# A seven-product scheme for the wide layers, with two of its weight sums made by accumulating DMAs

## The chip, the cores and the metric

One NeuronCore of a Trainium2 chip runs the program. The metric is the device time of one execution in microseconds, the median of several runs; a profile of one further execution gives the trace. TensorE is called PE, VectorE DVE, ScalarE ACT, GpSimd POOL and SyncE SP.

## The reference, cut to what matters

512 tokens of 1024 features go through two layers of a first block (projection, attention over selected keys, short convolution, gates, and an MLP) and then through a second block (projection, dilated attention, mLSTM, and a gated feed-forward network, here FFN). All is float32. The change touches the products of the MLP and of the FFN:

```python
for l in range(2):                                   # first block
    ...
    u = rmsnorm(x, norm_mlp[l])
    x = x + jnp.square(jax.nn.relu(u @ w_mlp_up[l])) @ w_mlp_down[l]   # 1024 -> 4096 -> 1024
...
h = modulate(rms_norm(x, g_ffn), sh_f, sc_f)          # second block
x = x + gt_f * ((jax.nn.silu(h @ w_gate) * (h @ w_up)) @ w_down)       # 1024 -> 2816 -> 1024
```

The vector by which the second block is modulated, `silu(c) @ w_ada + b_ada` with `w_ada` of 1024 x 6144, depends on none of this; the kernel computes it in pieces (`ada`) on DVE beside an MLP.

## The kernel before, in words

Activations are kept transposed: a tile has 128 features on the partitions and 512 tokens along the row, and x is eight such tiles. A large product is made exact enough by splitting both sides into two float32r parts. For the weights, `split` copies a raw tile of 4 x 128 rows by 256 columns (1024 elements in each partition) to `wh` on ACT (L171), and DVE subtracts that from the raw tile to get `wl` (L172). For the activations, `hilo` does the same with `hi` (L285, ACT) and `lo` (L286, DVE). Each block of 128 x 128 weights then takes three matmuls into one PSUM bank: wh by hi (L230), wh by lo (L231), wl by hi (L232). In the FFN, `gateup` has its own three (L1315 to L1317).

`linear` cuts a product into units (one split weight tile) and pieces (the matmuls of 128 output columns over 4 k-tiles of 128 rows), and calls an evacuation when a bank is complete. All pieces go into one list. `Prog.run` walks it in order: at a unit it emits the weight splits up to two units ahead, and a share of the background work ("bg", at "rate" pieces per unit; "drain" empties the rest); at a "do" it emits the work itself. A scheduler then orders the instructions of each engine, and every engine runs its own queue strictly in that order. Weights arrive on SP's queue in tiles of 1 MB (`fetch`, L161, three buffers). "Rate 0.8" lets the 48 `ada` pieces run as background in the MLP of layer 1.

The MLP goes in four chunks of 1024 hidden columns, in the order up 0, up 1, down 0, up 2, down 1, up 3, down 2, down 3. `rstd` comes after the first two pieces of up 0: a product of the square sums with a matrix of ones (L313), a root on ACT, a reciprocal and its refinement on DVE (L316 to L325). `evup` scales and clips on DVE (L732), squares on ACT (L733) and splits by `hilo`; `evdn` adds to x (L740), and after the last chunk `nextprep` splits x for the next stage. The last 512 output columns of layer 1 are made in two halves of 256 tokens (`parts_=2`), so that the norm of block 2 (L829 to L863) can begin on the first half. The FFN goes through `gateup` in groups of 256 columns, the first one in two token halves, and `down` in three chunks.

## Time and profile before

| | |
|---|---|
| median of 3 runs | 2069.94 us (2069.59 to 2069.95) |
| profiled execution | 2069.96 us, span 2067.9 us from first to last instruction |
| granted TensorE clock | 1.000 |
| PE busy | 2057.1 us, 99% of the span |
| DVE busy | 1260.0 us, 61% |
| ACT busy | 845.6 us, 41% |
| POOL busy | 19.7 us, 1% |
| HBM read | 211.55 MB |

How to read it: busy time is the union of an engine's instructions; a matmul's own duration overlaps the next one's, so what a matmul costs is the distance between two starts. A row of a timeline has the start and the length in us, the engine, the line of the kernel, the operation, its tiles (out<-in), its shape, and in brackets the idle time before it with what ended it. A group's row has the count, the busy time, and the mean of one in ns.

### The profile page before, as it was taken

What the parts mean: (1) busy time and instruction counts of PE and PEld (TensorE: products, weight loads), DVE (VectorE), ACT (ScalarE), POOL (GpSimd) and SP (SyncE); (2) the same over time, 40 slices, a digit from 0 to 9 for tenths busy, and PEclk for the clock granted to TensorE, in tenths of its full rate; (3) what the DMA queues carried; (4) which work ended last, traced back from release to release, by engine and by line L of the source; (5) the groups of instructions that cost most, each with busy time, mean ns of one, the idle gap of its engine ahead of it and who ended that gap; (6) DMA issues with size and microseconds to landing.
All of it is one profiled execution on the core that took longest, in us unless ns stands there. A gap on an engine that the chain in (4) does not pass through costs nothing.

```text
span 2067.9 us, 25080 instructions
## 1 busy us (share of the span) xinstructions
PE 2057.1 (99%) x9944; PEld 1700.7 (82%) x9944; DVE 1260.0 (61%) x2245; ACT 845.6 (41%) x1359; POOL 19.7 (1%) x33
## 2 busy tenths in 40 slices
PE   9999999999999999999999999999999999999999
PEld 7888888888888878888888888889877798888887
DVE  6999666644444569977657746567777375333333
ACT  5324773432322332238644322425377744322221
POOL 0000000000000000000000000000010000000000
PEclk9999999999999999999999999999999999999999
DMA  5222213233323222331134545452221123233231
GB/s 204 102 94 93 79 62 102 82 102 102 96 88 102 87 94 90 102 102 62 62 123 169 209 141 194 145 195 98 82 82 62 42 81 103 81 103 101 83 111 51
DMA packets 122148, 215.25 MB, mean 104 GB/s; under 512 B 5808, under 2 KB 30640, under 8 KB 122032
## 3 DMA queue, kind: packets, MB, share of 16 engines
q1 hardware_dynamic: 122032, 213.67, 30.9%
q8 instruction: 78, 1.28, 0.2%
q14 instruction: 38, 0.31, 0.0%
HBM read 211.55 MB, written 2.10 MB: 103 GB/s over the span
## 4 chain that ended last, share of the span: by engine, by line
PE 97%; DVE 1%; ACT 1%; issue 0%; DMA 0%; POOL 0%; SPq 0%; POOLq 0%; DVEq 0%; ACTq 0%
PE mm L230 25%; PE mm L232 25%; PE mm L231 25%; PE mm L1315 4%; PE mm L1317 4%; PE mm L1316 4%; PE at L352 1%; PE mm L260 1%; PE mm L261 1%; PE mm L262 1%; PE ot L386 1%; PE at L371 1%; PE at L1188 0%; PE at L1196 0%; PE at L582 0%
## 5 line engine op out<-in xcount | busy, mean ns | idle before, releaser
L230 PE MATMUL mm<-g,wh 128*128 128x512 f32 (+1 forms) x2400 | 919.5, 384 | 1.0 <-ACT wh L171 0.8
L232 PE MATMUL mm<-g,wl 128*128 128x512 f32 (+1 forms) x2400 | 916.0, 382 | 0.0
L231 PE MATMUL mm<-g,wh 128*128 128x512 f32 (+1 forms) x2400 | 915.4, 382 | 0.0
L171 ACT CAST wh<-raw 128x1024 fp32r<-128x1024 f32 (+2 forms) x356 | 366.4, 1032 | 825.8 <-PE mm L231 648.6
L172 DVE TENSOR_TENSOR wl<-raw,wh 128x1024 fp32r<-128x1024 f32 (+2 forms) x356 | 424.9, 1195 | 448.1 <-ACT wh L171 445.8
L230 PEld LDWEIGHTS mm<-g,wh 128*128 128x128 f32 x2400 | 450.4, 188 | 90.5 <-issue 4.3
L231 PEld LDWEIGHTS mm<-g,wh 128*128 128x128 f32 x2400 | 450.6, 188 | 86.3 <-issue 1.2
L232 PEld LDWEIGHTS mm<-g,wl 128*128 128x128 f32 x2400 | 450.7, 188 | 86.1
L1317 PE MATMUL mm<-g,wl 128*128 128x512 f32 (+1 forms) x384 | 142.6, 372 | 0.0
L1316 PE MATMUL mm<-g,wh 128*128 128x512 f32 (+1 forms) x384 | 142.4, 372 | 0.0
L1315 PE MATMUL mm<-g,wh 128*128 128x512 f32 (+1 forms) x384 | 142.2, 372 | 0.0
L286 DVE TENSOR_TENSOR g<-g,g 128x512 fp32r<-128x512 f32 x96 | 66.4, 691 | 49.7 <-ACT g L285 49.2
L285 ACT CAST g<-g 128x512 fp32r<-128x512 f32 x96 | 59.6, 621 | 60.6 <-DVE g L707 26.6
L1317 PEld LDWEIGHTS mm<-g,wl 128*128 128x128 f32 x384 | 72.3, 188 | 12.6
L1316 PEld LDWEIGHTS mm<-g,wh 128*128 128x128 f32 x384 | 72.3, 188 | 12.5
L1315 PEld LDWEIGHTS mm<-g,wh 128*128 128x128 f32 x384 | 72.1, 188 | 12.4
L740 DVE TENSOR_TENSOR x<-mm,x 128x512 f32<-128x512 f32 (+1 forms) x68 | 44.8, 658 | 56.5 <-PE mm L232 56.5
L803 DVE SCALAR_TENSOR_TENSOR g<-g,g 128x512 f32<-128x512 f32 x96 | 63.8, 688 | 8.6 <-DMA g<-w_ada 8.5
L733 ACT ACTIVATE g<-g 128x512 f32<-128x512 f32 x64 | 40.3, 630 | 70.1 <-DVE g L732 70.1
L360 ACT ACTIVATE g<-g,nm 128x128 f32<-128x128 f32 (+3 forms) x96 | 53.2, 555 | 17.8 <-DVE nm L355 17.1
L601 DVE MAX8 m<-g 128x8 f32<-128x256 f32 (+2 forms) x96 | 53.3, 558 | 1.9
L602 DVE MATCH_REPLACE8 g<-m,g 128x256 f32<-128x256 f32 (+2 forms) x96 | 52.1, 543 | 0.0
(222 smaller groups left out, 1574.4 us busy)
## 6 DMA issues: line engine op xcount, KB each, us to landing
raw<-w_in SPq DMA_DIRECT2D x53, 1024.0 KB, 5.0
raw<-w_mlp_up SPq DMA_DIRECT2D x32, 1024.0 KB, 5.4
raw<-w_mlp_down SPq DMA_DIRECT2D x32, 1024.0 KB, 5.1
g<-w_ada SPq DMA_DIRECT2D x96, 256.0 KB, 5.6
raw<-w_gate SPq DMA_DIRECT2D x11, 1024.0 KB, 5.1
raw<-w_up SPq DMA_DIRECT2D x11, 1024.0 KB, 5.2
raw<-w_down SPq DMA_DIRECT2D x10, 1024.0 KB, 5.0
raw<-w_mix_out SPq DMA_DIRECT2D x8, 1024.0 KB, 5.1
```

What stands on the lines that cost most here:

```text
L171: act.copy(hi, raw)
L172: dve.tensor_sub(lo, raw, hi.bitcast(F32))
L230: pe.matmul(ps, wh, hi[:, cs], start=st, stop=False)
L231: pe.matmul(ps, wh, lo[:, cs], start=False, stop=False)
L232: S["pe"] = pe.matmul(ps, wl, hi[:, cs], start=False, stop=en)
L285: act.copy(hi, src)
L286: dve.tensor_sub(lo, src, hi.bitcast(F32))
L601: dve.max(m8, acc[i][:, :W_])
L803: dve.scalar_tensor_tensor(w, w, 1.0, S["cb", n2], op0=ALU.mult, op1=ALU.mult, accum_out=modp[:, n2, n : n + 1])
L1315: pe.matmul(ps, wh, hi[:, cs], start=s == 0 and k_ == 0, stop=False)
L1316: pe.matmul(ps, wh, lo[:, cs], start=False, stop=False)
L1317: pe.matmul(ps, wl, hi[:, cs], start=False, stop=s == 1 and k_ == 3)
```

## The change

`seven` computes a block of 1024 rows by 512 weight columns as seven half-sized products in place of eight (the Strassen-Winograd form). The 1024 rows are cut into two halves and the 512 columns into two: four quarters a, b, c, d of 512 x 256; the tokens are cut into two halves of 256. Each of the seven products multiplies one quarter, or one sum of quarters, by one half of the tokens, or a mixture of them: 4 k-tiles x 2 column tiles x 3 matmuls of 256 columns. `mix` makes the eight mixture tiles (`ta`, `tb`) once for each MLP and for the FFN, as background work on DVE. Four sums of weights are needed in each block: a plus c (`ac`) and c plus d (`cd`) arrive by loading one quarter on SP's queue and adding the other onto the same tile with a DMA on POOL's queue; then DVE adds a (`p5`) and b (`p2`) to `cd` in place. The results are combined while they are evacuated (`e6`, `e7`, `keep`).

The blocks are 1 to 7 of eight in the up-projection of each MLP, and 2 to 10 of eleven in the FFN, where gate and up columns take the places of the two column halves: 23 in all. Their pieces are meshed with those of `down`, which now takes 512 hidden rows at a time, with weight tiles of 128 columns (`narrow`). Loads are cut to 0.5 MB and requested five units ahead (eight buffers), the `ada` pieces are spread over both layers, 24 each, at rate 0.25, and the rope tables are loaded per layer.

```diff
-    prog = Prog(split, 2)
+    prog = Prog(fetch, split, 5, 2)
...
+    def seven(srcs, xs, ta, tb, evac):
...
+        def of(name):
+            W, c0 = srcs["cd".count(name)]
+            r0 = 512 * "bd".count(name)
+            return W[r0 : r0 + 512, c0 : c0 + 256].rearrange("(k p) c -> p k c", p=P)
+
+        def get(*names):
+
+            def f():
+                for name in names:
+                    raw[name] = (ssp if name == "cd" else rawp).tile([P, 4, 256], F32, tag="ws" if name == "cd" else "raw", name=nm("raw"))
+                    nc.sync.dma_start(raw[name], of(name[0]))
+                    for more in name[1:]:
+                        nc.gpsimd.dma_start(raw[name], of(more), accum_op=ALU.add)
+            return f
+
+        def p5():
+            dve.tensor_add(raw["cd"], raw["cd"], raw["a"])
+
+        def p2():
+            dve.tensor_add(raw["cd"], raw["cd"], raw["b"])
+
+        us = {
+            1: {"load": get("a", "cd"), "make": lambda: raw["a"]},
+            5: {"load": get("b"), "make": lambda: raw["cd"], "post": p5},
+            6: {"load": get("ac"), "make": lambda: raw["cd"]},
+            2: {"load": get("d"), "make": lambda: raw["b"], "post": p2},
+            7: {"make": lambda: raw["ac"]},
+            3: {"make": lambda: raw["cd"]},
+            4: {"make": lambda: raw["d"]},
+        }
...
+        def e6():
+            u = tmp.pop(1)
+            dve.tensor_sub(u, bank["Y"], u)
+            dve.tensor_sub(bank["Z"], bank["Z"], u)
+            act.copy(bank["Y"], u)
...
+        def e7():
+            r = tmp.pop(5)
+            dve.tensor_sub(r, bank["Y"], r)
+            evac(1, 1, r, True)
...
+        prods = [
+            (1, "X", half(xs, 0, 0), keep(1, "X")),
+            (5, "Z", half(ta, 0, 0), keep(5, "Z")),
+            (6, "Y", half(tb, 0, 0), e6),
+            (2, "X", half(xs, 4, 0), e2),
+            (7, "Y", half(ta, 0, 1), e7),
+            (3, "Z", half(xs, 4, 1), e3),
+            (4, "Y", half(tb, 0, 1), e4),
+        ]
...
+                    ps = bank[b][:, th(m)]
+                    for k in range(4):
+                        hi, lo = mv(k)
+                        wh = u["hi"][:, k, m * P : (m + 1) * P]
+                        wl = u["lo"][:, k, m * P : (m + 1) * P]
+                        pe.matmul(ps, wh, hi, start=first and m == 0 and k == 0, stop=False, skip_group_check=True)
+                        pe.matmul(ps, wh, lo, start=False, stop=False, skip_group_check=True)
+                        S["pe"] = pe.matmul(ps, wl, hi, start=False, stop=k == 3, skip_group_check=True)
...
+    def mix(key, k, y):
...
+        def first():
+            y0, y1 = y(k), y(k + 4)
+            a_, b_ = st["a"], st["b"] = slot(), slot()
+            dve.tensor_sub(a_[:, th(0)], y0[:, th(0)], y0[:, th(1)])
+            dve.tensor_add(b_[:, th(0)], y1[:, th(1)], a_[:, th(0)])
+            dve.tensor_sub(a_[:, th(1)], y0[:, th(1)], y1[:, th(1)])
+            dve.tensor_sub(b_[:, th(1)], y1[:, th(0)], b_[:, th(0)])
...
+        def evup(c):
+            def f(n, t, src, own):
+                r = src if own else slot()
+                dve.scalar_tensor_tensor(two(r), two(src), 0.0, both(S["n", "rs"][:, th(t)]), op0=ALU.max, op1=ALU.mult)
                 S["act"] = act.activation(r, r, AF.Square)
-                hid[c, 4 * g + j] = hilo(r)
+                for m in range(2):
+                    k_ = 4 * c + 2 * n + m
...
+                    act.copy(hi[:, th(t)], r[:, th(m)])
+                    dve.tensor_sub(lo[:, th(t)], r[:, th(m)], hi[:, th(t)].bitcast(F32))
...
-        u0 = up(0)
+        u0 = linear(W_up, 0, [4, 4], 0, [P] * 4, xs, ev0)
         add(u0[:2])
         do(lambda: rstd("n"))
-        if l == 1:
-            do(ada_start)
-            I.append(("rate", 0.8))
-            I.append(("bg", [ada(n) for n in range(48)] + [ada_end]))
+        I.append(("rate", 2.5))
+        I.append(("bg", [f for k in range(4) for f in mix("n", k, y)]))
         add(u0[2:])
-        add(up(1))
-        add(down(0))
...
+        I.append(("drain", None))
+        do(ada_start)
+        I.append(("rate", 0.25))
+        I.append(("bg", [ada(n) for n in range(24 * l, 24 * l + 24)] + ([ada_end] if l else [])))
+        for c in range(1, NU):
+            I.extend(mesh(up(c), down(c - 1)))
...
+        u0 = gateup(0, 2)
...
+        I.append(("rate", 2.0))
+        I.append(("bg", [f for k in range(4) for f in mix("h", k, y)]))
+        add(gateup(1, 1))
+        I.append(("drain", None))
+        for c in range(2, NG - 1, 2):
+            I.extend(mesh(unit(c) + unit(c + 1), down(c // 2 - 1)))
+        I.extend(mesh(unit(NG - 1), down(ND - 2)))
+        add(down(ND - 1))
```

In the changed file the split is at L218 (both halves of `linear`'s three matmuls at L279 to L281), `hilo`'s low half at L456, `mix` at L476 to L479, `ev0` at L928, the three matmuls of `seven` at L401 to L403, and the accumulating DMA at L329.

Before, PE's queue in the MLP of layer 0 holds plain products of 512 columns. These rows are the third 128 columns of the second half of up 0 (numbers are the program's tile numbers, `g` are activations in halves):

```order
L230 MATMUL mm_3466<-g_3050,wh_3388 128x512
L231 MATMUL mm_3466<-g_3051,wh_3388 128x512
L232 MATMUL mm_3466<-g_3050,wl_3389 128x512
L230 MATMUL mm_3466<-g_3068,wh_3388 128x512
L231 MATMUL mm_3466<-g_3069,wh_3388 128x512
L232 MATMUL mm_3466<-g_3068,wl_3389 128x512
```

Now PE's queue has this a little later in that MLP, in the first `seven`: `mm_3648` and `mm_3700` are its products 5 and 6, `g_3570` and `g_3574` the high halves of the last mixtures `ta` and `tb`, `at_3630` the first tile of `down`, `g_3547` and `g_3566` the last two hidden tiles of `ev0`.

```order
L401 MATMUL mm_3700<-g_3518,wh_3644 128x256
L402 MATMUL mm_3700<-g_3519,wh_3644 128x256
L403 MATMUL mm_3700<-g_3518,wl_3645 128x256
L279 MATMUL at_3630<-g_3547,g_3510 128x512
L280 MATMUL at_3630<-g_3548,g_3510 128x512
L281 MATMUL at_3630<-g_3547,g_3511 128x512
L279 MATMUL at_3630<-g_3566,g_3510 128x512
L401 MATMUL mm_3648<-g_3570,wh_3586 128x256
L280 MATMUL at_3630<-g_3567,g_3510 128x512
L281 MATMUL at_3630<-g_3566,g_3511 128x512
L401 MATMUL mm_3700<-g_3574,wh_3644 128x256
```

Products of the mixtures and of the first hidden tiles alternate there, each with operands that DVE has just made.

DVE's queue at that place before the change: the end of `rstd`, then evacuations (L732), low halves (L286) and weight splits (L172).

```order
L324 SCALAR_TENSOR_TENSOR g_3305<-g_3306,g_3305 128x512
L325 SCALAR_TENSOR_TENSOR g_3307<-g_3305,g_3307 128x512
L732 SCALAR_TENSOR_TENSOR g_3362<-mm_3277,g_3307 128x512
L286 TENSOR_TENSOR g_3366<-g_3362,g_3365 128x512
L732 SCALAR_TENSOR_TENSOR g_3381<-mm_3290,g_3307 128x512
L172 TENSOR_TENSOR wl_3433<-raw_3430,wh_3432 128x1024
```

And now, the end of that stretch of DVE's queue, ahead of the operands in PE's rows:

```order
L456 TENSOR_TENSOR g_3515<-g_3463,g_3514 128x512
L456 TENSOR_TENSOR g_3519<-g_3464,g_3518 128x512
L476 TENSOR_TENSOR g_3526<-g_3522 128x256
L477 TENSOR_TENSOR g_3527<-g_3524,g_3526 128x256
L478 TENSOR_TENSOR g_3526<-g_3522,g_3524 128x256
L479 TENSOR_TENSOR g_3527<-g_3524,g_3527 128x256
L928 SCALAR_TENSOR_TENSOR g_3544<-mm_3411,g_3380 128x512
L456 TENSOR_TENSOR g_3548<-g_3544,g_3547 128x512
L928 SCALAR_TENSOR_TENSOR g_3563<-mm_3424,g_3380 128x512
L456 TENSOR_TENSOR g_3567<-g_3563,g_3566 128x512
L456 TENSOR_TENSOR g_3571<-g_3526,g_3570 128x512
L456 TENSOR_TENSOR g_3575<-g_3527,g_3574 128x512
```

From the first of `rstd`'s DVE instructions to the last of these, `g_3575`, DVE's listing has 44 rows: 16 of `mix`, 12 low halves, 4 wide weight splits, 2 weight sums, a narrow split, 4 evacuations and 5 of `rstd`.

POOL's queue had casts of the attention (L412 then, L600 now) and some memsets; now the accumulating DMAs stand between. The rows are those from the end of layer 0's MLP to the attention of layer 1; `raw_9853` and `raw_10432` are the `cd` tiles of layer 1's first two blocks.

```order
L329 DMA raw_5717<-w_mlp_up 128x4x256
L329 DMA raw_6024<-w_mlp_up 128x4x256
L329 DMA raw_6143<-w_mlp_up 128x4x256
L329 DMA raw_9853<-w_mlp_up 128x4x256
L329 DMA raw_10432<-w_mlp_up 128x4x256
L600 COPY g_7054<-g_7054 64x512
```

So these two sums of layer 1 are issued before its attention, with an SP load ahead of each.

## Rows read from the trace of the kernel before

**Rows 1.** the page: span, busy time by engine; the chain by engine
```profile
span 2067.9 us, 25080 instructions
...
PE 2057.1 (99%) x9944; PEld 1700.7 (82%) x9944; DVE 1260.0 (61%) x2245; ACT 845.6 (41%) x1359; POOL 19.7 (1%) x33
...
PE 97%; DVE 1%; ACT 1%; issue 0%; DMA 0%; POOL 0%; SPq 0%; POOLq 0%; DVEq 0%; ACTq 0%
```

**Rows 2.** products by shape: xcount | busy us, mean ns | idle before
```profile
L230 PE MATMUL mm<-g,wh 128*128 128x512 f32 x2192 | 858.8, 392 | 0.8 <-ACT wh L171 0.8
...
L1315 PE MATMUL mm<-g,wh 128*128 128x512 f32 x320 | 124.5, 389 | 0.0
...
L230 PE MATMUL mm<-g,wh 128*128 128x256 f32 x192 | 54.4, 286 | 0.2 <-ACT g L860 0.2
...
L1315 PE MATMUL mm<-g,wh 128*128 128x256 f32 x64 | 17.7, 284 | 0.0
```

**Rows 3.** timeline of PE, 1100 us: start, length; ends of 24 steps
```profile
1100.22 0.39 PE L230 MATMUL mm<-g,wh 128*128 128x512 f32 x1
...
1105.66 0.39 PE L230 MATMUL mm<-g,wh 128*128 128x512 f32 x1
```

**Rows 4.** timeline of PE at 1439 us: first and last of 35 steps
```profile
1439.03 0.28 PE L232 MATMUL mm<-g,wl 128*128 128x256 f32 x1
...
1443.23 0.28 PE L232 MATMUL mm<-g,wl 128*128 128x256 f32 x1
```

**Rows 5.** timeline of DVE at 1100 us, layer 1: start, length, operation, [idle before]
```profile
1100.92 0.69 DVE L286 TENSOR_TENSOR g<-g,g 128x512 fp32r<-128x512 f32 x1
1101.53 0.69 DVE L732 SCALAR_TENSOR_TENSOR g<-mm,g 128x512 f32<-128x512 f32 x1
1103.57 0.69 DVE L286 TENSOR_TENSOR g<-g,g 128x512 fp32r<-128x512 f32 x1 [1.35 <-ACT g L285]
...
1132.22 1.22 DVE L172 TENSOR_TENSOR wl<-raw,wh 128x1024 fp32r<-128x1024 f32 x1
1133.36 0.68 DVE L803 SCALAR_TENSOR_TENSOR g<-g,g 128x512 f32<-128x512 f32 x1
```

**Rows 6.** timeline at 1412 us: 256-column work, then the border
```profile
1412.43 0.42 DVE L740 TENSOR_TENSOR x<-mm,x 128x256 f32<-128x256 f32 x1
...
1412.76 0.41 DVE L307 TENSOR_TENSOR g<-g,g 128x256 f32<-128x256 f32 x1
...
1415.54 0.58 PE L829 MATMUL at<-rdc,g 128*128 128x1 f32 x4
...
1421.50 0.48 DVE L863 SCALAR_TENSOR_TENSOR g<-g,modc,g 128x256 fp32r<-128x256 f32 x1
```

**Rows 7.** high half of a split on ACT: xcount, mean ns
```profile
L171 ACT CAST wh<-raw 128x1024 fp32r<-128x1024 f32 x342 | 359.6, 1053 | 802.8 <-PE mm L231 627.4 <-PE mm L1316 81.0 <-issue 71.4
```

**Rows 8.** stretches: length, then busy PE, PEld, DVE, ACT, POOL; clock, DMA, GB/s
```profile
65.00:235.00 170.00, 169.95 (x762) 140.74 (x760) 153.33 (x303) 61.84 (x89) 2.45 (x4) 1.00 0.30 99
415.00:700.00 285.00, 285.00 (x1259) 236.07 (x1258) 120.19 (x136) 89.78 (x109) 0.00 (x0) 1.00 0.30 98
1125.00:1415.00 290.00, 290.00 (x1332) 242.40 (x1331) 175.90 (x322) 93.00 (x118) 0.32 (x1) 1.00 0.50 174
```

**Rows 9.** timeline of DVE where the MLP of layer 0 begins
```profile
374.36 0.69 DVE L316 TENSOR_SCALAR g<-at 128x512 f32<-128x512 f32 x1 [0.77 <-ACT g L315]
...
381.61 0.69 DVE L732 SCALAR_TENSOR_TENSOR g<-mm,g 128x512 f32<-128x512 f32 x1
```

**Rows 10.** timeline of PE at the same place
```profile
371.27 1.02 PE L313 MATMUL at<-g,kon 128*128 128x512 f32 x2
```

**Rows 11.** busy time in slices where the FFN begins
```profile
1720.00:1730.00 10.00, 10.00 (x72) 9.39 (x71) 6.56 (x11) 4.64 (x8) 0.00 (x0) 1.00 0.29 93
1730.00:1740.00 10.00, 10.00 (x46) 8.28 (x45) 2.45 (x2) 2.11 (x2) 0.00 (x0) 1.00 0.37 119
```

**Rows 12.** DMA issues: xcount, KB each, median us from issue to landing
```profile
raw<-w_mlp_up SPq DMA_DIRECT2D x32, 1024.0 KB, 5.4
```

More of the change, by code (lines that the diff above doesn't have):

```diff
@@ L26 @@
 FF2 = 2816
+MLP_TILES = 32
+FF_TILES = FF2 // P
 C_NMIX, C_NMLP, C_NFIN, C_GMIX, C_GFFN = 0, 16, 32, 40, 48
@@ L48, with __init__ @@
 class Prog:
-    def __init__(self, split, ahead):
+    def __init__(self, fetch, split, early, ahead):
         self.items = []
+        self.fetch = fetch
         self.split = split
+        self.early = early
         self.ahead = ahead
@@ L64, in run @@
             if kind == "unit":
+                while got < len(units) and got <= cur + self.early:
+                    self.fetch(units[got])
+                    got += 1
                 while nxt < len(units) and nxt <= cur + self.ahead:
@@ L98, in interleave, with mesh @@
     return out
+def mesh(a, b):
+    n = len(a)
+    out = []
+    for i, x in enumerate(a):
+        out.extend(x)
+        for p in b[i * len(b) // n : (i + 1) * len(b) // n]:
+            out.extend(p)
+    return out
 @with_exitstack
@@ L162, in fetch, with granule @@
         return raw
-    def split(u):
-        chunk, k0, kn, cc0, ccn = u["src"]
-        if id(chunk) not in raws:
-            raws[id(chunk)] = fetch(chunk)
-        raw = raws[id(chunk)][:, k0 : k0 + kn, cc0 : cc0 + ccn]
-        hi = whp.tile([P, kn, ccn], F32R, tag="wh", name=nm("wh"))
-        lo = whp.tile([P, kn, ccn], F32R, tag="wl", name=nm("wl"))
+    def granule(u):
+        ch, k0, kn, cc0, ccn = u["src"]
+        W, r0, kt, c0, cw = ch
+        if kt * cw <= GRAN:
+            return (id(ch), 0, 0), (W, r0, kt, c0, cw)
+        gw = min(max(ccn, GRAN // kn), cw - cc0 // (GRAN // kn) * (GRAN // kn))
+        g0 = cc0 // (GRAN // kn) * (GRAN // kn)
+        return (id(ch), k0, g0), (W, r0 + k0 * P, kn, c0 + g0, gw)
+    def fetch(u):
+        if "load" in u:
+            u["load"]()
+        if "src" in u:
+            key, what = granule(u)
+            if key not in raws:
+                raws[key] = load(*what)
+    def split(u):
+        if "make" in u:
+            raw = u["make"]()
+            kn, ccn = raw.shape[1:]
+        else:
+            ch, k0, kn, cc0, ccn = u["src"]
+            key, what = granule(u)
+            k0, cc0 = (k0, cc0) if key[1:] == (0, 0) and what[2] * what[4] == ch[2] * ch[4] else (0, cc0 - key[2])
+            raw = raws[key][:, k0 : k0 + kn, cc0 : cc0 + ccn]
+        if u.get("narrow"):
+            hi, lo = (slot(F32R, kn * ccn).rearrange("p (k c) -> p k c", k=kn) for _ in range(2))
+        else:
+            hi = whp.tile([P, kn, ccn], F32R, tag="wh", name=nm("wh"))
+            lo = whp.tile([P, kn, ccn], F32R, tag="wl", name=nm("wl"))
         act.copy(hi, raw)
@@ L203, in linear @@
             ch = chunk(W, row0 + kbase * P, kt, c0, cw)
-            us = halves(ch)
+            us = halves(ch, narrow)
             steps.append((kbase, kt, us))
@@ L237, in linear, with th, two, both @@
                         first = False
+        return pieces
+    def th(t):
+        return slice(t * H, (t + 1) * H)
+    def two(ap):
+        return ap.rearrange("p (n c) -> p n c", n=2)
+    def both(ap):
+        return ap.unsqueeze(1).to_broadcast([P, 2, H])
+    def seven(srcs, xs, ta, tb, evac):
+        raw = {}
+        bank = {}
+        tmp = {}
+        def of(name):
[23 more added lines that the diff above has]
+        }
+        def half(d, k0, t):
+            return lambda k: [o[:, th(t)] for o in d(k0 + k)]
+        def keep(n, b):
+            def f():
+                tmp[n] = slot()
+                act.copy(tmp[n], bank[b])
+            return f
+        def e6():
[3 more added lines that the diff above has]
+            act.copy(bank["Y"], u)
+        def e2():
+            evac(0, 0, bank.pop("X"), False)
+        def e7():
+            r = tmp.pop(5)
+            dve.tensor_sub(r, bank["Y"], r)
+            evac(1, 1, r, True)
+        def e3():
+            evac(0, 1, bank.pop("Z"), False)
+        def e4():
+            evac(1, 0, bank.pop("Y"), False)
+        prods = [
[7 more added lines that the diff above has]
+        ]
+        pieces = []
+        for n, b, mv, after in prods:
+            first = n in (1, 5, 6)
+            u = us[n]
+            piece = [("unit", u)]
+            for m in range(2):
+                def emit(u=u, b=b, mv=mv, m=m, first=first):
+                    if first and m == 0:
+                        bank[b] = mmbank()
+                    ps = bank[b][:, th(m)]
[6 more added lines that the diff above has]
+                        S["pe"] = pe.matmul(ps, wl, hi, start=False, stop=k == 3, skip_group_check=True)
+                piece.append(("do", emit))
+            piece.append(("do", after))
+            pieces.append(piece)
@@ L1351, in down, with y @@
             p = []
[L1352 removed]
+            kt = min(4, FF_TILES - 4 * c)
+            last = c == ND - 1
             for g in range(2):
[L1354 removed]
+                p += linear(a["w_down_2"], 512 * c, [kt], 512 * g, [P] * 4, lambda k_: ff[4 * c + k_], evff(c, g),
+                            narrow=not last, newbank=mmbank if last else atbank)
             def free():
[L1357 to L1358 removed]
+                for k_ in range(kt):
+                    ff.pop(4 * c + k_)
             p.append([("do", free)])
             return p
[L1363 removed]
+        def y(j):
+            t = slot()
+            hi, lo = S["h", j]
+            dve.tensor_add(t, hi.bitcast(F32), lo.bitcast(F32))
+            return t
+        u0 = gateup(0, 2)
         add(u0[:8])
```

165 lines of the change are left out of this document (102 added, 63 removed).

## The prediction

> **What bounds the kernel now.** I read the page first: TensorE (PE) is busy for 2057.1 of the 2067.9 us of the span, and the chain that ended last is 97% PE [rows 1]. So only fewer or shorter products, or new waits of PE, can move the time. Second, the products by shape: most have 512 moving columns, the rest here 256 [rows 2]. Their means (392 and 286 ns) overlap in the pipeline, so the price is the distance between starts. At 1100 us, 24 steps take 5.44 us, 0.2267 us each [rows 3]. At 1439 us, 35 steps with 256 columns take 4.20 us, 0.120 us each [rows 4]. Two half products cost 0.240 us, 6% more than a whole one. Third, the stretches: in both MLPs PE never idles, while VectorE (DVE) is busy for 120 of 285 us and 176 of 290 us, ScalarE (ACT) for 90 and 93; the granted clock is 1.00 throughout [rows 8]. The new work must fit into that DVE and ACT room. That DVE can be full without hurting PE is seen in the attention stretch (153.3 of 170 us, PE 169.95) [rows 8], but that work was not all awaited by PE.
>
> **The products.** A block of 1024 rows by 512 columns takes 96 products of 512 columns now: 96 x 0.2267 = 21.76 us. `seven` takes 7 x 24 = 168 of 256 columns: 168 x 0.120 = 20.16 us. The gain is 1.60 us, not an eighth (2.72), since halves are dearer. There are 23 such blocks (7 in each layer, 9 in the FFN): 36.9 us. Around them 48 more whole products stay in 512 columns that ran as 96 halves, since fewer pieces are cut in two token halves (-0.6 us). In sum 2160 products of 512 and 96 of 256 columns go, 3864 of 256 come: -489.7 - 11.5 + 463.7 = **-37.5 us**.
>
> The rows give 226.7 and 120.0 ns [rows 3, 4]. The Trainium skill (TensorE: Matmul & The Clock Gate, Back-to-back issue gap) gives the isolated gap as N/2.4 + 2.5 ns, 215.8 and 109.2 ns; by it the sum would be about -54.7 us. The trace has 11 ns more on either shape, which weighs double on halves, so I keep the rows.
>
> **The steady iteration.** One `seven` meshed with one `down` piece of 512 hidden rows keeps PE for 20.16 + 21.76 = 41.9 us. DVE by distance between starts: 1.14 us for 1024 wide (1132.22 to 1133.36), 0.61 for 512 (1100.92 to 1101.53) [rows 5], 0.33 for 256 [rows 6], of which I take 0.36. Seven splits and two sums of weights 10.3; eight narrow splits 4.9; e6 and e7 1.8; `evup` 4 x 0.61 + 8 x 0.36 = 5.3; eight adds to x 4.9; 3.4 pieces of ada at two 0.61 each 4.2: 31.4 us of 41.9. ACT has seven casts of 1.05 [rows 7] and some 22 shorter operations, about 20 us. Both fit. But DVE waits in order: where a result makes the round trip DVE, ACT, DVE with nothing between, it idles 1.35 us [rows 5]. Following the order of one iteration, the narrow splits come just in time. I take 0.15 us per iteration, **+2 us** for 14 (bounds 0 and 7).
>
> **The start of each MLP** is the dearest new wait. Before, DVE needs only the four evacuations there. Now, between the reciprocal root and the first `seven`, the same queue carries `mix`, weight sums and `ev0`. In layer 0 DVE starts on it at 374.36; the root takes 7.25 us to 381.61, 1.14 of it a split [rows 9], so 6.1. Then come 16 operations of 256 columns (5.8), 12 low halves of 512 (7.3), 4 splits and 2 sums of 1024 (6.8), a narrow split (0.6), and 4 evacuations (2.4): with the root 29.0 us, to 403.4 without a gap. Four round trips, at up to 1.35 us [rows 5], add 5: 408.4. PE finishes the rstd products at 372.3 [rows 10], then has 72 products of 0.2267 (to 388.6), 58 of 0.120 and 12 of 0.2267 (to 398.3), where the listing has it wait for the last `ta` and `tb` from DVE. The wait is 5 us without gaps and 10 with them. Queued behind it on PE are the `down` products, which wait for `ev0` in the same DVE queue, so nothing can fill the hole. I take 10 for each layer, **+20 us** (bounds 10 and 24), since the evacuations there are the same round trips as that in [rows 5].
>
> **The borders.** Layer 1 to block 2: the second token half of the last `down` covers the norm of the first. Eight pieces of 12 x 0.120 are 11.5 us now; with four k instead of eight, 5.8. The first normalised tile takes from 1415.54 to 1421.98 [rows 6], 6.4 us, and seven more follow: about +2.5. Layer 0 to 1: in the last `down` a tile of x is finished every 2.72 us, in place of four close together, a pause, and four more; DVE needs some 2.4 us for each (add, low half, square sum, half a split), which leaves little to catch up with: +1.5. Together **+4 us** (0 to 9).
>
> **The start of the FFN.** `mix` takes 8 adds, 16 short operations and 8 low halves, 15.6 us, plus 4.6 for the first `seven`'s splits and sum; DVE idles 3.4 + 7.6 = 11 us in the 20 us concerned [rows 11]. The surplus of 9 is partly covered by the first product, which needs no mixture, and the `down` pieces between: **+3 us** (0 to 8).
>
> **Loads.** An iteration moves 5 x 0.5 MB by plain loads and 2 x 0.5 by accumulating ones, 2 MB for `down` and 1.7 for ada: 7.2 MB in 41.9 us, 172 GB/s, which layer 1 sustains now (174, PE full) [rows 8]. No accumulating transfer stands in the trace. The nearest row is a 1 MB load, 5.4 us to landing [rows 12]. `ac` is requested five units (of 2.8 us) ahead of product 6 and cast for product 7 some seven units later, 20 us; minus the load 15 are left for the sum. `cd` is requested far earlier, as POOL's listing shows. Even at twice a load both are hidden, so I take 0 (bounds 0, and what the second rival gives). POOL itself is 1% busy [rows 1].
>
> **Sum**: -37.5 + 2 + 20 + 4 + 3 = -8.5 us against the profiled execution's 2069.96 (span 2067.9 and 2.1 around it; the median of the runs is 2069.94, the same): **2061.5 us**. All lower bounds give -27.5 (2042.5), all upper ones +10.5 (2080.5).
>
> **Rivals.** *The full gain*: DVE gets to `mix` early enough, or the round trips fill each other, and the starts cost under 5 us each. For it: some low halves run without any gap, as the one at 1100.92 [rows 5], and the listing mixes the chains. Against: 29 us of work stand in a window of 24 (374.36 to 398.3). Time 2032 to 2042. *DVE becomes the bound of every iteration* (slower): four evacuations and eight late narrow splits, each followed by an idle of 0.8 to 1.35 us, add 10 to 12 us to the 31.4 and the iteration takes 43 to 44.5 instead of 41.9. It decides from 42.5 (8.5 us over 14); at 44.5 it costs 36 instead of 2: 2096. For it speaks the idle of 1.35 [rows 5]; against it that ada and splits stand between the steps of a round trip in the listing. *The accumulating sum is late*: every us beyond the 15 stops ACT's cast, the squares queued behind it, and so PE, 23 times. Landing at 16 us instead of 15 takes +23 (2084); the point is 15.4. Against: 5.4 us for a plain load of twice the size [rows 12].
>
> The Trainium skill (SBUF — State Buffer, SBUF: two separate sides) warns that a DMA issued from GpSimd starves while DVE runs a two-port operation. Its section Who interferes with whom says that tensor_tensor has no two-port mode, and by that rule the DVE work here would not delay the sums. No run here shows either yet.
>
> **Chances.** The forecast with its bounds (2042.5 to 2080.5) 68%: 54 faster, 9 within 0.2% (2065.8 to 2074.1, about what a measurement here can tell from no change), 5 slower. Full gain 12%, DVE the bound 13%, late sums 7%. So faster 0.66, same 0.09, slower 0.25. The range 2039 to 2084 leaves out half of the first rival and most of the other two, about 18%.
>
> **What would show it.** Right: 3864 products at L401 to L403, 0.120 us apart; a hole of about 10 us on PE, ahead of L401 and L279, waiting for L456, some 26 us after the rstd products of each MLP, and hardly any PE idle in the later iterations; accumulating transfers landing within 10 us; PE idle of 1 to 5 us at the two borders and the FFN's start. Wrong: no hole at the starts (then 2042 or less); PE idle repeated in every iteration with DVE named (then above 2080); PE waiting for casts that wait for a POOL transfer; or halves that run at another distance than 0.120, each ns of which is 3.9 us.

## The result: slower by 1.0%, and the profile after

The changed kernel takes 2089.57 us (2088.61 to 2093.44), against 2069.87 for the kernel before: 1.0099 times as long, 95% interval 1.0081 to 1.0116. The forecast was 2061.5, with a range up to 2084.

The page of the changed kernel: span, busy time, PE's busy tenths and its granted clock in 40 slices, and the chain that ended last:

```profile
span 2087.3 us, 29797 instructions
...
PE 2044.1 (98%) x11552; PEld 1757.9 (84%) x11552; DVE 1525.6 (73%) x2755; ACT 982.7 (47%) x1699; POOL 79.2 (4%) x79
...
PE   9999999899999999999998999999999998999999
...
PEclk9999999899999999999999999999999998999999
...
PE 87%; DVE 7%; DMA 3%; ACT 2%; issue 1%; SPq 0%; POOL 0%; ACTq 0%; DVEq 0%; POOLq 0%
```

PE is busy for 13 us less than in [rows 1], yet the span is 19.4 us longer, and the chain is no longer PE's alone. PE is busy for eight tenths in three slices, the starts of the two MLPs and of the FFN, and in the first and the last of these the mean clock falls too. PE's longest waits (us in total, times, longest):

```profile
PE mm L401 <- DVE g L928: 12.6, 4, 4.1
PE at L1056 <- DVE g L1054: 6.8, 3, 4.0
PE mm L1533 <- ACT g L217: 5.4, 2, 4.1
PE at L281 <- DVE g L218: 3.0, 5, 1.6
```

These four add up to 27.8 us, most of it in the three slices (2.8 of the 6.8 us on L1054 lie at the border to block 2); with the clock behind them and the order of PE's work more is lost than they show. To see in which stage it lies, I take the starts of the `rstd` products (L501) in both MLPs and of the next stage, of the first product of block 2 that gives tokens by features (L430), and of the norm's column sums ahead of the FFN (L1045):

```profile
371.48 1.02 PE L501 MATMUL at<-g,kon 128*128 128x512 f32 x2
...
745.68 1.02 PE L501 MATMUL at<-g,kon 128*128 128x512 f32 x2
...
1086.38 1.02 PE L501 MATMUL at<-g,kon 128*128 128x512 f32 x2
...
1497.67 0.39 PE L430 MATMUL mm<-wh,g 128*128 128x512 f32 x1
...
1709.39 0.61 PE L1045 MATMUL at<-rdc,g 128*128 128x1 f32 x4
```

| stage (us) | before | after | longer by | products alone | so lost |
|---|---|---|---|---|---|
| MLP of layer 0, rstd to rstd | 368.1 | 374.2 | 6.1 | -11.2 | 17.3 |
| MLP of layer 1 and border, rstd to L430 | 398.9 | 411.3 | 12.4 | -11.8 | 24.2 |
| column sums to the end (FFN) | 377.0 | 377.9 | 0.9 | -14.4 | 15.3 |

All else is equal within 0.4 us. The columns "before" come from the same products in the trace before (L313 at 371.27 [rows 10], 739.37 and 1080.28, L260 at 1479.15, L829 at 1690.85, the end of the span).

The steady iterations are as forecast. These are the first products (L401) of the second, third and fourth block of layer 0:

```profile
445.86 0.28 PE L401 MATMUL mm<-g,wh 128*128 128x256 f32 x1
...
488.56 0.28 PE L401 MATMUL mm<-g,wh 128*128 128x256 f32 x1
...
530.61 0.28 PE L401 MATMUL mm<-g,wh 128*128 128x256 f32 x1
```

From one block's first L401 to the next one's is 42.05 to 42.14 us in the middle of both MLPs (worked out: 41.9) and 42.4 to 42.7 at their ends, in the FFN 31.1 (31.04); starts on PE are 0.120 and 0.227 us apart as in [rows 3, 4]. So the products do give back 37 us. What is lost sits at the starts. In layer 0 the second block begins at 445.9, 74.4 us after the `rstd` products; at these paces the work between takes 59.2 (1.0, 72 x 0.2267, 41.9): 15.2 us lost. In layer 1 it begins at 1162.0, 75.6 us after: 16.4 lost.

The stretch in layer 0, first PE (start, length, operation, idle before and what ended it), then DVE, then both in slices:

```profile
388.48 0.39 PE L281 MATMUL mm<-g,wl 128*128 128x512 f32 x1
392.92 0.55 PE L401 MATMUL mm<-g,wh 128*128 128x256 f32 x1 [4.06 <-DVE g L928]
...
393.48 0.41 PE L403 MATMUL mm<-g,wl 128*128 128x256 f32 x1
...
397.96 0.33 PE L403 MATMUL mm<-g,wl 128*128 128x256 f32 x1
...
403.90 0.39 PE L401 MATMUL mm<-g,wh 128*128 128x256 f32 x1 [2.23 <-DVE g L928]
...
412.32 0.28 PE L402 MATMUL mm<-g,wh 128*128 128x256 f32 x1
```

```profile
374.58 0.69 DVE L504 TENSOR_SCALAR g<-at 128x512 f32<-128x512 f32 x1 [0.78 <-ACT g L503]
...
392.09 0.68 DVE L928 SCALAR_TENSOR_TENSOR g<-mm,g 128x512 f32<-128x512 f32 x1
...
396.76 0.69 DVE L456 TENSOR_TENSOR g<-g,g 128x512 fp32r<-128x512 f32 x1 [1.35 <-ACT g L455]
...
405.20 0.69 DVE L456 TENSOR_TENSOR g<-g,g 128x512 fp32r<-128x512 f32 x1 [1.35 <-ACT g L455]
...
407.84 1.90 DVE L456 TENSOR_TENSOR g<-g,g 128x512 fp32r<-128x512 f32 x3 [1.35 <-ACT g L455]
```

```profile
core 0: us, PE busy (x) PEld busy (x) DVE busy (x) ACT busy (x) POOL busy (x), PEclk, DMA share, GB/s
380.00:390.00 10.00, 8.87 (x40) 7.00 (x38) 9.97 (x17) 5.86 (x9) 0.00 (x0) 1.00 0.17 52
390.00:400.00 10.00, 7.08 (x35) 6.85 (x36) 6.41 (x12) 5.82 (x10) 0.00 (x0) 0.66 0.17 55
400.00:410.00 10.00, 6.39 (x25) 4.32 (x24) 7.08 (x14) 6.07 (x11) 0.00 (x0) 0.74 0.48 157
450.00:700.00 250.00, 249.49 (x1559) 225.16 (x1558) 188.23 (x317) 106.88 (x178) 14.18 (x11) 1.00 0.64 178
```

PE has finished the first plain block at 388.9 and waits 4.06 us for L928, the evacuation of `ev0`, since four PSUM banks are full; then its products run 0.213 us apart (393.48 to 397.96 in 21 steps) in place of 0.120, at the lower of the clock's two levels, 1.2 GHz; the mean of the slice from 390 is 0.66. Then it waits 0.68 us for a mixture's low half (at 401.17), 2.23 us for L928 again, which frees the bank of product 6, and 0.69 us for the high half of a hidden tile (at 407.86). The two waits for L928, here and in layer 1, are the 12.6 us above. DVE works through the queue shown ahead of the prediction from 374.58 to 409.74, with an idle of 1.02 us after the first L928 and of 1.35 us, as in [rows 5], after the other three. In the slices to 410 it is nearly full at first and then waits for ACT's round trips; PE is busy for 6.4 to 8.9 of 10 us. From 450 on PE is busy for 249.5 of 250 us with DVE at 75%.

The FFN's start, PE, then ACT and one line of DVE:

```profile
1723.78 0.61 PE L1045 MATMUL at<-rdc,g 128*128 128x1 f32 x4
1728.36 1.19 PE L1056 MATMUL at<-g,kon 128*128 128x256 f32 x2 [3.97 <-DVE g L1054]
1733.65 0.58 PE L1533 MATMUL mm<-g,g 128*128 128x256 f32 x1 [4.11 <-ACT g L217]
```

```profile
1721.08 1.05 ACT L217 CAST wh<-raw 128x1024 fp32r<-128x1024 f32 x1 [0.79 <-DVE raw L333]
...
1724.79 1.03 ACT L217 CAST wh<-raw 128x1024 fp32r<-128x1024 f32 x1
...
1731.79 1.31 ACT L1076 ACTIVATE g<-g,modc 128x256 fp32r<-128x256 f32 x3 [1.07 <-DVE g L1066]
1733.00 0.60 ACT L217 CAST g<-raw 128x512 fp32r<-128x512 f32 x1
```

```profile
1725.00 1.22 DVE L336 TENSOR_TENSOR raw<-raw,raw 128x1024 f32<-128x1024 f32 x1
```

PE waits 3.97 us for the norm's diagonal (L1054) and 4.11 us for a narrow weight split (L217, 512 wide, at 1733.00). The two casts of 1024 at 1721 and 1724 belong to the first `seven`, like two more at 1711.38 and 1714.96: they are made ahead of the splits that PE needs first. On DVE that block's second sum (L336) and a low half (L218, 1.22 us at 1726.21) stand ahead of the norm's refinement, and the diagonal comes late. The late narrow split follows in ACT's queue on the norm's own operations (L1076), which wait for DVE; it comes some 7 us after the last of the wide casts has ended.

The accumulating DMAs: their queue (packets, MB, share of 16 engines), and beside a plain load their issues (xcount, KB, median us to landing):

```profile
q0 software_dynamic: 24288, 24.12, 7.5%
...
raw<-w_mlp_up SPq DMA_DIRECT2D x78, 512.0 KB, 3.9
...
raw<-w_mlp_up POOLq DMA_DIRECT2D x28, 512.0 KB, 9.8
```

They land in 9.8 us for `w_mlp_up` (a plain load of the same size in 3.9); PE's and ACT's longest waits name none of them.

### The profile page after: what moved, and what is told of

Read it like the earlier page. It is cut to its first block, busy times and chain, and to the rows that moved or that the text cites. A ratio compares the mean times of both kernels' runs of the same rounds, so it can differ in the third digit from the quotient of the medians.

```text
span 2087.3 us, 29797 instructions
## 1 busy us (share of the span) xinstructions
PE 2044.1 (98%) x11552; PEld 1757.9 (84%) x11552; DVE 1525.6 (73%) x2755; ACT 982.7 (47%) x1699; POOL 79.2 (4%) x79
## 4 chain that ended last, share of the span: by engine, by line
PE 87%; DVE 7%; DMA 3%; ACT 2%; issue 1%; SPq 0%; POOL 0%; ACTq 0%; DVEq 0%; POOLq 0%
PE mm L279 13%; PE mm L280 13%; PE mm L281 13%; PE mm L401 7%; PE mm L402 7%; PE mm L403 6%; PE at L281 6%; PE at L279 6%; PE at L280 6%; DMA g<-w_ada 3%; PE at L540 1%; DVE wl L218 1%; PE ot L574 1%; PE mm L430 1%; PE mm L431 1%; PE mm L432 1%
## 5 line engine op out<-in xcount | busy, mean ns | idle before, releaser
L217 ACT CAST wh<-raw 128x1024 fp32r<-128x1024 f32 (+2 forms) x341 | 349.8, 1028 | 741.3 <-PE mm L402 350.2
L218 DVE TENSOR_TENSOR wl<-raw,wh 128x1024 fp32r<-128x1024 f32 (+2 forms) x341 | 406.0, 1192 | 215.6 <-ACT wh L217 213.7
L279 PE MATMUL mm<-g,wh 128*128 128x512 f32 (+2 forms) x1328 | 506.9, 383 | 1.6 <-ACT g L1076 1.6
L281 PE MATMUL mm<-g,wl 128*128 128x512 f32 (+2 forms) x1328 | 503.9, 380 | 0.0
L280 PE MATMUL mm<-g,wh 128*128 128x512 f32 (+2 forms) x1328 | 502.9, 379 | 0.0
L401 PE MATMUL mm<-g,wh 128*128 128x256 f32 x1288 | 367.1, 285 | 14.9 <-DVE g L928 12.6
L402 PE MATMUL mm<-g,wh 128*128 128x256 f32 x1288 | 367.2, 285 | 1.3 <-DVE g L456 1.3
L403 PE MATMUL mm<-g,wl 128*128 128x256 f32 x1288 | 366.9, 285 | 0.0
L279 PEld LDWEIGHTS mm<-g,wh 128*128 128x128 f32 (+1 forms) x1328 | 250.3, 189 | 51.6 <-issue 4.3
L281 PEld LDWEIGHTS mm<-g,wl 128*128 128x128 f32 (+1 forms) x1328 | 250.3, 189 | 46.0 <-DVE wl L218 0.4
L280 PEld LDWEIGHTS mm<-g,wh 128*128 128x128 f32 (+1 forms) x1328 | 250.4, 189 | 45.7 <-issue 1.2
L401 PEld LDWEIGHTS mm<-g,wh 128*128 128x128 f32 x1288 | 249.3, 194 | 22.4 <-issue 8.9
L402 PEld LDWEIGHTS mm<-g,wh 128*128 128x128 f32 x1288 | 249.2, 193 | 7.3 <-DVE g L456 1.7
L403 PEld LDWEIGHTS mm<-g,wl 128*128 128x128 f32 x1288 | 249.4, 194 | 0.3
L281 PE MATMUL at<-g,g 128*128 128x512 f32 x608 | 238.3, 392 | 3.0 <-DVE g L218 3.0
L279 PE MATMUL at<-g,g 128*128 128x512 f32 x608 | 239.7, 394 | 1.2 <-ACT g L455 1.2
L280 PE MATMUL at<-g,g 128*128 128x512 f32 x608 | 239.2, 393 | 0.0
L281 PEld LDWEIGHTS at<-g,g 128*128 128x128 f32 x608 | 114.6, 188 | 30.7 <-DVE g L218 6.3
L279 PEld LDWEIGHTS at<-g,g 128*128 128x128 f32 x608 | 115.0, 189 | 22.2 <-ACT g L455 2.7
L280 PEld LDWEIGHTS at<-g,g 128*128 128x128 f32 x608 | 115.0, 189 | 19.1 <-DVE g L456 0.4
L218 DVE TENSOR_TENSOR g<-raw,g 128x512 fp32r<-128x512 f32 x168 | 113.1, 684 | 11.7 <-ACT g L217 11.7
L217 ACT CAST g<-raw 128x512 fp32r<-128x512 f32 x168 | 100.2, 617 | 0.0
```

The source lines that it names most:

```text
L217: act.copy(hi, raw)
L218: dve.tensor_sub(lo, raw, hi.bitcast(F32))
L279: pe.matmul(ps, wh, hi[:, cs], start=st, stop=False)
L280: pe.matmul(ps, wh, lo[:, cs], start=False, stop=False)
L281: S["pe"] = pe.matmul(ps, wl, hi[:, cs], start=False, stop=en)
L401: pe.matmul(ps, wh, hi, start=first and m == 0 and k == 0, stop=False, skip_group_check=True)
```

## The experiments

All medians beside the kernel before on the same chip, 2069.9 to 2070.1. The stages of each, in the order of the table above, rstd to rstd, rstd to L430 (or its line there), column sums to the end:

| kernel | median us | ratio, 95% | layer 0 | layer 1 | FFN |
|---|---|---|---|---|---|
| changed | 2089.6 | 1.0081 to 1.0116 | 374.2 | 411.3 | 377.9 |
| four sums on DVE | 2086.2 | 1.0064 to 1.0094 | 371.8 | 410.4 | 378.0 |
| plain eight | 2087.0 | 1.0068 to 1.0098 | 368.5 | 406.5 | 385.3 |
| late seven | 2062.2 | 0.9946 to 0.9975 | 360.8 | 401.2 | 378.1 |
| wide units in the FFN | 2074.5 | 1.0015 to 1.0034 | 371.3 | 412.1 | 363.4 |
| idle products | 2088.7 | 1.0077 to 1.0105 | 372.7 | 412.5 | 377.9 |
| other banks | 2085.8 | 1.0065 to 1.0090 | 373.1 | 409.3 | 378.8 |
| early mixtures | 2079.1 | 1.0033 to 1.0058 | 370.3 | 407.4 | 378.2 |
| border | 2083.2 | 1.0050 to 1.0080 | 373.1 | 406.1 | 377.8 |
| combined | 2042.4 | 0.9856 to 0.9883 | 360.5 | 393.0 | 363.5 |
| combined, short lead | 2041.7 | 0.9849 to 0.9882 | 360.3 | 392.2 | 363.5 |
| combined, sums on DVE | 2039.7 | 0.9838 to 0.9868 | 359.7 | 390.4 | 363.5 |

**Four sums on DVE, no accumulating DMA.**

```diff
-            1: {"load": get("a", "cd"), "make": lambda: raw["a"]},
-            5: {"load": get("b"), "make": lambda: raw["cd"], "post": p5},
-            6: {"load": get("ac"), "make": lambda: raw["cd"]},
-            2: {"load": get("d"), "make": lambda: raw["b"], "post": p2},
+            1: {"load": get("a", "c", "d"), "make": lambda: raw["a"]},
+            5: {"load": get("b"), "make": sums, "post": p5},
+            6: {"make": lambda: raw["cd"]},
+            2: {"make": lambda: raw["b"], "post": p2},
...
+        def sums():
...
+            dve.tensor_add(raw["ac"], raw["a"], raw["c"])
+            dve.tensor_add(raw["cd"], raw["c"], raw["d"])
```

> All four weight sums of a block are made on DVE from plain loads of a, b, c and d; no accumulating DMA is left, and a block loads 2 MB in place of 3.5. Theory (the 57 us that the profile after has beside the products lie in the three starts, on DVE's queue): DVE gets two more sums of 1.14 us per block, which the steady iteration hides (33.7 of 42), so the time stays within 5 us of the changed kernel, 2087 to 2094. Rival (the accumulating transfers, 6 to 10 us to landing, hold the splits up): the time falls by 10 us or more, below 2080.

Measured 2086.2, 3.3 less than the changed kernel and 0.8 below the theory's band, far from the rival's. The two MLP stages are 2.4 and 0.9 us shorter, the FFN 0.1 longer. So the accumulating DMAs are not what makes the kernel slower; they gain nothing either.

**Plain eight products in the changed frame.** `up(c)` and `unit(c)` are replaced by plain `linear` and `gateup` pieces, and `mix` is left out.

```diff
-            I.extend(mesh(up(c), down(c - 1)))
+            I.extend(mesh(plain(c), down(c - 1)))
...
-            I.extend(mesh(unit(c) + unit(c + 1), down(c // 2 - 1)))
+            I.extend(mesh(gateup(c, 1) + gateup(c + 1, 1), down(c // 2 - 1)))
...
```

> The changed kernel with all its rearrangement (narrow weight tiles, loads of 0.5 MB, meshed pieces of 512 hidden rows, ada in both layers), but with eight plain products of 512 columns in each block and no mixtures. Theory: the holes at the two MLP starts are those of the mixtures and go, the steady iteration takes 43.5 us; what stays are the border to block 2 (6 us) and part of the FFN's start (4 to 9): 2078 to 2085. Rival (the rearrangement itself is dear, the seven products gain what was worked out): 37 us above the changed kernel, 2115 or more.

Measured 2087.0, 2 above the theory's band and far from the rival's. Layer 0 takes 368.5 us, as before (368.1): the frame costs nothing there, and the 15 us are the seven's. Layer 1 is 7.6 longer and the FFN 8.3: these two losses need no seven-product form. The frame costs 17 us, more than I had put down for it. The FFN's start in it, PE and ACT (line numbers are 5 higher here):

```profile
1716.72 0.67 PE L1061 MATMUL at<-g,kon 128*128 128x256 f32 x2 [0.54 <-DVE g L1059]
1722.02 0.58 PE L1538 MATMUL mm<-g,g 128*128 128x256 f32 x1 [4.63 <-ACT g L217]
```

```profile
1720.15 1.31 ACT L1081 ACTIVATE g<-g,modc 128x256 fp32r<-128x256 f32 x3 [1.07 <-DVE g L1071]
1721.36 0.60 ACT L217 CAST g<-raw 128x512 fp32r<-128x512 f32 x1
```

The wait for the norm's diagonal, 3.97 us in the changed kernel, is down to 0.54, but PE waits as long as there for a narrow split, and its products run 0.213 us apart for some 5 us after that. No `seven` and no wide cast stands ahead of that split; the norm's own operations (L1081) do.

**Late seven.** The second up block is plain too; the mixtures get 43 us more of PE's work beside them.

```diff
-        I.append(("rate", 2.5))
+        I.append(("rate", 0.7))
...
         add(u0[2:])
+        I.extend(mesh(plain(1), down(0)))
         I.append(("drain", None))
...
-        for c in range(1, NU):
+        for c in range(2, NU):
```

> The first two up blocks of each MLP are plain, the second one meshed with down 0, and the mixtures are made in the background over both; the seven-product form begins with the third block (6 per MLP instead of 7). Theory: with 43.5 us more of PE's work beside it DVE makes the mixtures in time, the holes of 15 and 16 us go but for 0 to 6 us in all, two blocks less cost 3.2 us: 2061 to 2068. Rival (the first block in the seven-product form starts late wherever it stands, by its bank, its sums or its evacuations): above 2083.

In this one the later mixtures are made of an x to which `down(0)` has already added, so it computes other values with the same instructions; `ada` runs at rate 0.3. Measured 2062.2, in the theory's band: layer 0 gets 13.4 us shorter than in the changed kernel though it has one block less in the cheap form, layer 1 10.1.

**Wide units in the FFN's plain groups.**

```diff
-            us = {
-                (w, s, j): {"src": (ch, 4 * s, 4, P * j, P), "narrow": True}
-                for s in range(2) for w, ch in (("g", chg), ("u", chu)) for j in range(2)
-            }
+            us = {(w, s): {"src": (ch, 4 * s, 4, 0, 256)} for s in range(2) for w, ch in (("g", chg), ("u", chu))}
...
```

> The plain gate and up groups at the FFN's start use weight units of 256 columns from the pool of split weights, as the kernel before does, in place of tiles of 128 columns from the slots. Theory: the hole of 9 us there (1724 to 1734) has its cause in the late narrow splits, queued behind the splits and sums of the first seven; it shrinks to under 3 us: 2080 to 2084. Rival (the mixtures fill DVE and the hole is theirs): within 2 us of the changed kernel.

Measured 2074.5, 15 less, more than expected (the band began at 2080). PE's longest waits in it:

```profile
PE mm L401 <- DVE g L928: 12.6, 4, 4.1
PE at L1056 <- DVE g L1054: 3.0, 3, 1.9
```

The wait for the split (L1533 on L217, 5.4 us) is gone, that for the norm's diagonal is down from 6.8 to 3.0 (of the 3.97 us at the FFN's start 0.17 are left), and the FFN takes 363.4 us, 13.7 less than in the kernel before; the products alone are 14.4. The mixtures are still made there: they cost under 1 us.

**Idle products that keep the clock up.** 34, 20 and 20 products of 256 columns into a bank that nothing reads, at the holes of each MLP's start.

```diff
+                for _ in range(n):
+                    pe.matmul(ps[:, :H], z[:, :P], z[:, :H], start=True, stop=True)
...
+                u[0] = u[0][:1] + [busy(34)] + u[0][1:] + [busy(20)]
+                u[1] = u[1] + [busy(20)]
```

> The changed kernel with 74 idle products of 256 columns, into a bank that nothing reads, put in PE's queue at the holes of each MLP's start (34 before the first product in the seven-product form, 20 after it, 20 in the next), 8.9 us of work on PE at the pace of 0.12. If the low granted clock after the hole (0.66 and 0.74 between 390 and 410 us, 24 products at 0.213 in place of 0.120) is itself part of the loss: PE keeps its full clock and the time falls by 4 to 10 us, 2080 to 2086. If DVE's queue sets the start (its last low half ends at 409.7 whatever PE does): within 2 us of the changed kernel, 2088 to 2092.

Measured 2088.7, 0.8 less. The slices of layer 0's start there (columns as above):

```profile
380.00:390.00 10.00, 10.00 (x51) 8.48 (x50) 9.97 (x17) 5.84 (x9) 0.00 (x0) 1.00 0.17 54
390.00:400.00 10.00, 10.00 (x81) 9.71 (x80) 7.34 (x13) 6.81 (x12) 0.00 (x0) 1.00 0.20 62
400.00:410.00 10.00, 8.58 (x50) 7.21 (x49) 7.12 (x14) 4.91 (x9) 0.00 (x0) 0.91 0.44 150
```

The clock stays at 1.00 up to 400 us and 0.91 after, where it was 0.66 and 0.74; layer 0 gets 1.5 us shorter and layer 1 1.2 longer. The Trainium skill (TensorE: Matmul & The Clock Gate, Part 1, What's actually happening) says that an idle PE is throttled to half and that activity releases it; both traces agree. But here the low clock after the first wait follows from the wait for DVE and costs almost nothing by itself. The products behind DVE's last low half ran 0.213 us apart in this trace too (409.41 to 411.33), so what the clock costs there was not tried.

**Other banks for the first plain block.**

```diff
+        order = iter([atbank, atbank, mmbank, mmbank])
-        u0 = linear(W_up, 0, [4, 4], 0, [P] * 4, xs, ev0)
+        u0 = linear(W_up, 0, [4, 4], 0, [P] * 4, xs, ev0, newbank=lambda: next(order)())
```

> Two of the four PSUM banks of the first plain up block are taken from the other pool, so that the first product in the seven-product form finds a free bank and needn't wait for ev0 (the wait of 4.06 us at 388.5). If the bank is what costs there: 4 us less per MLP, 2080 to 2083. If DVE's queue sets the start: the wait only moves behind the first product, within 2 us of the changed kernel.

Measured 2085.8, 3.8 less, between the two bands. The wait for the bank shrinks from 12.6 to 1.2 us, and another takes its place (below it the operation on ACT that stands before that split):

```profile
PE at L279 <- ACT g L217: 10.7, 4, 4.9
...
PE mm L401 <- DVE g L928: 1.2, 2, 0.6
```

```profile
395.61 0.63 ACT L929 ACTIVATE g<-g 128x512 f32<-128x512 f32 x1 [1.39 <-DVE g L928]
```

PE now waits 4.87 us for a weight split of `down` that ACT makes at 396.79, behind the square and the high half of a tile of `ev0`, for which ACT itself waited on DVE. The bank is a small part of the loss (1.1 us in layer 0, 2.0 in layer 1).

**Early mixtures.** The background work is put ahead of the first two pieces.

```diff
+        I.append(("rate", 2.5))
+        I.append(("bg", [f for k in range(4) for f in mix("n", k, y)]))
         add(u0[:2])
         do(lambda: rstd("n"))
-        I.append(("rate", 2.5))
-        I.append(("bg", [f for k in range(4) for f in mix("n", k, y)]))
```

> The mixtures, which need x and not the reciprocal root, may start one unit earlier, ahead of the first two pieces of up 0. If DVE's queue sets the start: each us of mixture work that is done before the root at 374.6 comes off both starts, 2 to 5 us each: 2080 to 2086. If bank or clock set it: within 2 us of the changed kernel.

Measured 2079.1, 10.5 less by the medians and 0.9 below the band; 3.9 us come off each of the two MLP stages by the profiles. Moving DVE's work forward is what helps.

**Border.** In both MLPs the second 512 output columns of the last two chunks of hidden rows are taken together.

```diff
-            for g in range(2):
-                p += linear(a["w_mlp_down"][l], 512 * c, [4], 512 * g, ...
+            for g in range(1 if c == NU - 2 else 2):
+                c_ = NU - 2 if last and g == 1 else c
+                p += linear(a["w_mlp_down"][l], 512 * c_, [4] * (c - c_ + 1), 512 * g, ...
```

> One edit alone on the changed kernel: in both MLPs the last 512 output columns are taken over the last two chunks of hidden rows at once, as before, so that the second token half covers 11.5 us in place of 5.8 at the border to block 2. Theory (the loss of 6 us at that border is the halved cover): layer 1's MLP and border get 4 to 6 us shorter, the median is 2083 to 2086. Rival (the loss there has another cause, such as DVE's backlog from the last block): within 2 us of the changed kernel's 2089.6.

Measured 2083.2, in the theory's band; layer 1 with its border gets 5.2 us shorter, layer 0, which has no second half there, 1.1. The edit also spares DVE four additions to x in each layer, so that not all of the 5.2 need be the cover.

**Combined.** Late seven (with the plain second block and `down(0)` each by itself, so that the mixtures are done before x changes), wide units, and border.

```diff
-        I.append(("rate", 2.5))
+        I.append(("rate", 1.2))
...
+        add(plain(1))
         I.append(("drain", None))
...
+        add(down(0))
-        for c in range(1, NU):
+        for c in range(2, NU):
...
```

> Three edits: the first two up blocks of each MLP are plain, the mixtures are made beside both and before down 0 (6 blocks in the seven-product form per MLP); the FFN's plain groups use units of 256 columns from the pool of split weights; and the last 512 output columns of the MLP are taken over the last two chunks of hidden rows at once, as before, so that the second token half covers 11.5 us at the border to block 2. Theory (three starts and one border hold the loss): from 2089.6, 31.6 less for the two starts, 3.2 more for two blocks, 15 less in the FFN, 5 less at the border: 2041, and 0 to 8 for what is left of them: 2041 to 2049. Rival (the loss moves to the next block that starts, DVE being full): above 2060.

Measured 2042.4, in the theory's band: 0.9869 of the kernel before, and 47 us less than the changed one, where the three edits alone gave 27.4, 15.1 and 6.4. Two of its longest waits of PE:

```profile
PE at L559 <- DVE nm L543: 2.0, 3, 0.9
...
PE at L1070 <- DVE g L1068: 1.3, 2, 1.2
```

The first is in the attention and as long as before, the second, 1.2 us of it, at the border to block 2. No wait at the start of an MLP or of the FFN is left among the longest.

**Combined with all sums on DVE**, the first experiment's edit on this version.

> The combined kernel with all four weight sums on DVE and no accumulating DMA (the first experiment's edit on the version without holes). Theory (the accumulating DMAs are hidden, 6 to 12 us to landing, and DVE has room for two more sums of 1.14 us per block in the steady iteration): within 3 us of the combined kernel, 2039.5 to 2045.5. Rival A (the accumulating DMAs cost something even there): 2036 or less. Rival B (DVE becomes the bound with 33.7 of 42 us): above 2050.

Measured 2039.7, 2.7 less than with the accumulating DMAs, just inside the theory's band; it is the fastest of all, 0.9853 of the kernel before, though the intervals of the two ratios overlap. Its slices, at the start of layer 0's MLP and in its middle:

```profile
380.00:410.00 30.00, 30.00 (x134) 24.82 (x133) 24.01 (x42) 19.72 (x31) 0.00 (x0) 1.00 0.17 53
450.00:700.00 250.00, 250.00 (x1538) 225.12 (x1537) 200.19 (x328) 109.05 (x178) 0.00 (x0) 1.00 0.45 141
```

PE never idles in these stretches; DVE is busy for 80% in the steady part.

**Combined, with a shorter lead.**

```diff
-    prog = Prog(fetch, split, 5, 2)
+    prog = Prog(fetch, split, 3, 2)
```

> The combined kernel with loads, and so the accumulating DMAs, requested three units ahead instead of five, some 5.6 us less. If the sums have little to spare (20 us from request to cast, minus 4 for the load and 6 to 12 for the sum): waits of ACT's cast for the transfer appear in many blocks and the time rises by 5 to 40 us, 2047 to 2082. If there is ample slack, because the queues run ahead of the list: within 3 us of the combined kernel, 2039.5 to 2045.5.

Measured 2041.7, no change. The queues run ahead of the list, and the transfers have slack at both leads.

## Why the prediction was wrong

**The products** (-37.5): right. Paces and steady iterations are as read from [rows 3, 4], and the FFN with wide units keeps 13.7 of its 14.4 us.

**The steady iteration** (+2, bounds 0 and 7): 3.9 in both MLPs and 0.6 in the FFN, what their distances of 42.05 to 42.7 and 31.1 us have beyond 41.9 and 31.04.

**The start of each MLP** (+20, bounds 10 and 24): the right place, engine and mechanism, and too small; 31.6 us were lost (15.2 and 16.4). DVE's walk was good: its last low half ended at 409.74, forecast 408.4. What failed is the step from there to PE. I let PE do all 70 products but the last two rows ahead of that moment and put the wait at the end. In the trace PE is past the same products at 412.3 where 398.3 was worked out, because its queue stopped earlier as well: first for a PSUM bank (4.06 us), which I had not counted at all, then for a mixture (0.68), for a second bank (2.23) and for a hidden tile (0.69), and 14 of the 70 products were still to be done when DVE had finished, at the lower clock. So of the 5 us beyond the forecast 10, DVE's later end holds 1.3, these products 2.6, and what lies behind them the rest (0.64 of it a wait for a narrow split at 437.82). Other banks and idle products show that neither the bank (3.8 us by the medians) nor the clock after the first wait (0.8) is the cause by itself; early mixtures (-10.5), the late seven (-27) and plain eight, whose layer 0 is as long as before, show that it is the work added to DVE's queue (the mixtures, and the first block's splits and sums), which stands ahead of or among the evacuations of `ev0`.

**The borders** (+4, 0 to 9): 6.0 at the border to block 2 instead of 2.5, and the cause as named, the halved cover: restoring it took 5.2 us off. At the border between the layers, forecast at 1.5, nothing is lost: the start (15.2) and the steady iterations (2.1) make up layer 0's 17.3.

**The start of the FFN** (+3, bounds 0 and 8): 14.7, the second term that failed, and for another reason than I gave. The mixtures cost under 1 us there. The loss is that with narrow units the plain groups' splits come late: in plain eight, with no `seven` at all, that alone makes PE wait 4.63 us and the FFN 8.3 longer than before. The first seven's splits and sums, which are made ahead of them, add the late diagonal (3.97 us instead of 0.54); the rest (1.33 of it a second wait for a narrow split, at 1775.49) was not taken apart. With wide units both waits go, and the FFN keeps all but 0.7 us of the products' gain. I had priced the change of `gateup` to narrow units at nothing and followed DVE's sum of work there, not the order of ACT's queue. Why the narrow splits come late in that order was not tried.

**The rivals**: the accumulating DMAs late (7%) did not happen, DVE as the bound of every iteration (13%) and the full gain (12%) did not either. The result came from the forecast's own terms, two of them beyond their upper bounds: 31.6 + 14.7 + 6.0 + 4.5 = 56.8 against -37.5, or 19.3 of the 19.4 measured on the span.

**Where the expected gain went**: it was there in every steady block and was spent at three starts, where work of DVE or ACT stands ahead of what PE needs next, and at one border.

## What to carry to other kernels

A scheme that trades products for additions is paid for where it starts: price the start by walking the queues of every engine up to the first steady block, and count banks and the order of the splits, not only the sum of the added work. Let the expensive form begin one block later, beside plain work that covers its preparation: it cost 3.2 us of the gain here and gave back some 30. Before such a scheme is called a loss, look at the distance between two blocks in the middle: if that is as worked out, the loss is at the edges and can be mended.
